# Where the rotary tables' loads stand in the preparation of a two-layer encoder trunk

## The chip, the cores and the metric

The kernel runs on one core of a Trainium2 chip. The metric is the device time of one execution in microseconds (us). Before the change it is 1481.55 us, the median of three runs (1478.82, 1481.55 and 1482.13). The engines are called as in the profile: PE is TensorE's matmul, PEld its weight load, DVE is VectorE, ACT is ScalarE, POOL is GpSimd, and SP is SyncE, which computes nothing here and issues nearly all DMAs. Each engine has a queue of its own and works it off in its written order; semaphores hold an instruction back until what it needs is there.

## The reference

The kernel computes a trunk of two encoder layers over 1024 tokens of width 1024, with a memory of 256 tokens. What matters for this change is the first layer's input side:

```python
memn = rmsnorm(mem, mem_norm_gain)
h = rmsnorm(x, norm_gain[l])
mk, mv = jnp.split(memn @ w_mem_kv[l], 2, axis=-1)
qa, ka, va, qb, kb, vb, qm, gate = split_cols(h @ w_in_even[e], SPLIT_EVEN)
qa = rope_2d(rmsnorm(qa.reshape(B, S, A_HEADS, HEAD_DIM), q_norm_a[e]), grid_row, grid_col)
ka = rope_2d(rmsnorm(ka.reshape(B, S, A_KV, HEAD_DIM), k_norm_a[e]), grid_row, grid_col)
ya = global_gqa(qa, ka, va.reshape(B, S, A_KV, HEAD_DIM))
```

`rope_2d` turns each half of a head's 64 numbers by angles that depend on the token's row and column of a 64-wide grid. The kernel doesn't compute the angles: tables of their cosines and sines (128 x 8 x 64 numbers each) are inputs, and so are the gains of the per-head norms. The rest of the layer (a global, a windowed and a memory attention, a gate, an output projection), the second layer and the final norm come after the stage that is changed.

## The kernel before

**Number format.** All products are made of 32-bit numbers split in two parts. A weight tile is loaded raw; ScalarE copies it to the high part (`wh`, L125 by way of `wparts`), VectorE or GpSimd subtracts that from the raw tile to get the low part (`wl`, L160), and TensorE makes three matmuls of each product (high by high, high by low, low by high).

**The preparation** is `project_a` (the phase named "prep"). In the order of the program it does this:

- `quarter(q, ...)` for q = 0 to 3 loads the transposed tokens a quarter at a time (`x<-xq`, L956), multiplies them by the norm's gain and splits them; `a_unit(ws, q)` multiplies a quarter by the weights of A's keys and values (L864). `quarter(4, ...)` does the same for the transposed memory (`x<-mq`). The last of these loads is kept in `self.loaded`.
- `mem_keys(w0, ...)` makes the memory's keys of layer 0: four heads of two weight units each, eight units in all, two heads to a PSUM bank (`pj`, then `tr`; matmuls at L568). `mem_values(w0, ...)` makes the values from eight more units (matmuls at L597).
- `rope_tables()` loads the factors (`so<-g_kq`, L777: four rows of 64 numbers spread over all partitions) and the two tables (`rt<-c_cos` and `rqn<-c_sin`, both L781), and GpSimd multiplies each table by the key's and by the query's factors (L784, four instructions on 128 x 512 numbers). The results, `c_cosk`, `c_cosq`, `c_sink` and `c_sinq`, are read by `rope` (L893, L895) for each quarter of keys and queries.
- `rstd(io["mt"], ...)` loads the token-major memory in four pieces (`xt<-mt`, L814; a tag of three buffers), squares and sums each on ScalarE (L815), and makes 1 / rms of the memory's tokens. `mem_keys` and `mem_values` are finished with it.
- `a_weights(1)` loads and splits the weights of A's first queries: two units into buffers of the tag `x` (L844), two into `wraw`. `stats(range(4))` does for the first four blocks of the token-major x what `rstd` does for the memory (`xt<-xt`, L814, eight pieces).
- Then follow the evictions, the rotary embedding of keys (`k_unit`) and queries (`q_unit`), the second layer's memory keys and values, and the other statistics.

**What sets the order.** The framework's planner sorts the instructions of each engine ahead of time: it runs a model of the chip, and gives each engine, whenever it is free there, the ready instruction that comes first by program order; `ahead("w")` moves a weight unit's load and split 40 places forward. A load is ready only when its buffer is free in that model. The order so found is the order in which the engine runs on the chip, where each instruction waits for its semaphores. The raw weight tiles share four buffers (`wraw`), and so do the high and the low parts (`wh`, `wl`), so a unit's load waits for the split of the unit four places before.

**`behind()`** is the only thing that was written by hand about the order of these loads: inside it, an instruction on SyncE is placed behind `self.loaded` in SyncE's queue (an order in the queue, no wait). `wload` appends each raw load to `self.raws`. The first four (`raws[0]` to `raws[3]`) are the weights of A's keys and values, and `raws[4]` to `raws[11]` are the eight units of the memory's keys. So `raws[6]` is their third and `raws[9]` their sixth. The lines around the change are in `project_a`; `rope_tables`, `rstd`, `a_weights` and `wload` all read `self.loaded` at the moment when they are traced.

Of the kernel before, what the change touches and what calls it, by code (L numbers as in the profile page):

```python
# [64 lines left out]
class Trunk:  # L65
# [881 lines left out]
    def project_a(self, qa, ks, v, qd, mem_h, kvd):  # L947


        nc, tc, io = self.nc, self.tc, self.io  # L950

        def quarter(q, parts, kps=range(4)):
            for kp in kps:
                x = self.st("x", [128, 2, 256], pool=self.xp)
                src = io["xq"][q, kp] if q < 4 else io["mq"][kp]
                loaded = nc.sync.dma_start(x, src.rearrange("p (a n) -> p a n", a=2))  # L956
                for i in range(2):
                    kt = 2 * kp + i
                    self.with_gain(x[:, i, :], kt + (0 if q < 4 else 16), *parts(kt))
            return loaded  # L960

        def tokens(q):
            return lambda kt: tuple(t[kt][:, q * 256:(q + 1) * 256] for t in self.h)
        late = []

        def after(end):

            late.append(end)
            if len(late) > 1:
                flush()  # L970

        def flush():
            with tc.issue_after(self.last.ins):
                late.pop(0)()

        warm = self.st("rp", [128, 512], F32R)
        self.st("so", [128, 512])
        self.st("rt1", [128, 512])
        nc.gpsimd.memset(warm.bitcast(F32), 0.0)
        nc.scalar.activation(self.rs_m, warm.bitcast(F32)[:, :2], AF.Sqrt)  # L980
        p = [self.ps("pj") for _ in range(2)]
        for i in range(9):
            nc.tensor.matmul(p[i % 2], warm[:, :128], warm, start=True, stop=True)
        w0, w1m = io["w_mem0"], io["w_mem1"]
        mem_l = self.st("mem", [128, KT, MEM], F32R, pool=self.xp)
        mem = [[t[:, i, :] for t in mem_h for i in range(4)], [mem_l[:, i, :] for i in range(KT)]]
        ws = self.a_weights(0, lambda kp: quarter(0, tokens(0), [kp]))
        units = []
        for q in range(4):
            units.append(self.a_unit(ws, q))  # L990
            if q < 3:
                quarter(q + 1, tokens(q + 1))
        self.loaded = quarter(4, lambda kt: (mem[0][kt], mem[1][kt]))
        for q, a in enumerate(units):
            units[q] = self.st("x", [128, 2, 256], pool=self.xp)
            self.copy(units[q], a)
        self.wsplit = ("act", "dve")
        end = [self.mem_keys(w0, mem, kvd[0], ("pj", "tr"), "so", "rt1")]
        self.wsplit = ("act", "both")
        end.append(self.mem_values(w0, mem, kvd[0], "so"))  # L1000
        self.rope_tables()
        vm = self.st("xv", [128, 2])
        self.loaded = self.raws[6]
        self.rstd(io["mt"], [0, 1], vm, self.rs_m)
        self.wsplit = ("act", "dve")
        w1 = self.a_weights(1)
        self.stats(range(4))
        self.loaded = None
        self.along_columns(self.rows_m, self.rs_m)
        for e in end:  # L1010
            e()
        for q in range(2):
            after(self.k_unit(units[q], q, ks, v))
        self.mem_keys(w1m, mem, kvd[1], ("tr", "tr"), "so", "rt1")()
        self.stats(range(4, 8))
        for q in range(2, 4):
            after(self.k_unit(units[q], q, ks, v))
        for q in range(4):
            after(self.q_unit(self.a_unit(w1, q), q, 0, qa, qd))
        w2 = self.a_weights(2)  # L1020
        self.along_columns(self.rows, self.rs)
        for q in range(4):
            after(self.q_unit(self.a_unit(w2, q), q, 2, qa, qd))
            if q == 1:
                self.mem_values(w1m, mem, kvd[1], "so")()
        while late:
            flush()
        return self.mem_q(io["w_e"], E_QM)
# [1239 lines left out]
```

## Time and profile before

| what | value |
|---|---|
| median of three runs | 1481.55 us |
| the profiled execution's own time | 1482.22 us |
| its span, from the first to the last instruction | 1480.4 us |
| TensorE busy | 1461.3 us (99%) |
| VectorE busy | 1038.8 us (70%) |
| ScalarE busy | 839.2 us (57%) |
| GpSimd busy | 647.0 us (44%) |
| moved by DMA | 271.87 MB, 184 GB/s in the mean |
| granted TensorE clock | 0.998 |

The profile is one execution of the program, taken by the hardware's profiler. Its page gives busy times for the whole span. For a single stage one asks the trace for smaller things: the busy time of each engine in chosen stretches, what an engine waited for, and the instructions of one engine in order of time. In such a row the first number is the start in us from the beginning of the span, the second how long it took (several equal instructions in a row are merged, with their count behind an x), and the brackets tell how long the engine had been idle before and which instruction or DMA ended that. For SyncE a row is the issue of a DMA, not its transfer; a view of DMA issues gives the time from the issue to the landing. A matmul's end is modelled, so that matmuls overlap in the rows; what counts is when they start.

### The profile page before, as it was taken

The numbers are of one execution on the slowest core, as the hardware profiler recorded it, in microseconds if no ns is written. First come the engines' busy times: TensorE is split into PE (matmuls) and PEld (weight loads), VectorE is DVE, ScalarE is ACT, GpSimd is POOL, SyncE is SP. The second block draws the span as 40 slices with busy tenths as digits, with TensorE's granted clock in tenths as the row PEclk, the third lists the DMA queues.
The fourth block names the chain that finished last, engine by engine and source line by source line (L and its number), as shares of the span: only waits on it lengthen the run. The fifth ranks groups of instructions, "written<-read, shape, count | busy, mean of one in ns | idle before, by whom it ended". The sixth has DMA issues, their size and how long they took to land.

```text
span 1480.4 us, 24751 instructions
## 1 busy us (share of the span) xinstructions
PE 1461.3 (99%) x8049; PEld 1254.1 (85%) x8049; DVE 1038.8 (70%) x2125; ACT 839.2 (57%) x1877; POOL 647.0 (44%) x766
## 2 busy tenths in 40 slices
PE   9999999999999999999999999999999999999997
PEld 8898888888888888888888887888888888888776
DVE  6687777777776678776687866654457787778584
ACT  7743665556655466655454544444456777776454
POOL 1223658566775656553450000002425556665355
PEclk9999999999999999999999999999999999999999
DMA  8966335334342524378553343567675568778844
GB/s 282 314 161 184 117 114 168 122 122 132 117 144 79 199 75 139 110 263 313 182 180 135 136 136 139 156 171 256 225 257 169 187 198 270 246 250 313 306 132 150
DMA packets 171809, 271.87 MB, mean 184 GB/s; under 512 B 15648, under 2 KB 92704, under 8 KB 170656
## 3 DMA queue, kind: packets, MB, share of 16 engines
q1 hardware_dynamic: 171248, 270.20, 56.6%
q8 instruction: 64, 1.05, 0.3%
q14 instruction: 65, 0.53, 0.1%
q10 hardware_dynamic: 432, 0.09, 0.0%
HBM read 174.28 MB, written 83.89 MB: 174 GB/s over the span
## 4 chain that ended last, share of the span: by engine, by line
PE 87%; DMA 4%; DVE 4%; ACT 2%; issue 1%; SPq 1%; POOL 0%; DVEq 0%; ACTq 0%; POOLq 0%
PE pj L242 16%; PE pj L62 12%; PE x L1650 7%; PE tr L133 6%; PE pv L1080 4%; PE y L1650 4%; PE pv L62 3%; PE s L62 3%; PE sa L1348 3%; PE tr L62 3%; PE pj L1348 2%; PE pv L1650 2%; PE sa L1046 2%; PE sa L1047 2%; PE s L1348 2%; PE tr L1348 2%
## 5 line engine op out<-in xcount | busy, mean ns | idle before, releaser
L549 DVE TENSOR_TENSOR pl<-tr,ph 128x512 fp32r<-128x512 f32 (+2 forms) x352 | 204.3, 594 | 45.2 <-ACT ph L125 43.3
L242 PE MATMUL pj<-H,wh 128*128 128x512 f32 x704 | 233.4, 412 | 0.4 <-DVE vt L313 0.2
L125 ACT ACTIVATE ph<-tr 128x512 fp32r<-128x512 f32 (+2 forms) x352 | 176.8, 523 | 99.6 <-PE tr L133 77.8
L158 POOL TENSOR_SCALAR wh<-wraw 128x512 fp32r<-128x512 f32 x48 | 30.4, 636 | 268.0 <-PE x L1650 233.2
L125 ACT ACTIVATE wh<-wraw 128x384 fp32r<-128x384 f32 (+1 forms) x163 | 89.2, 554 | 98.5 <-PE pj L1348 11.8
L242 PE MATMUL pj<-H,wl 128*128 128x512 f32 x352 | 139.0, 395 | 0.0
L242 PEld LDWEIGHTS pj<-H,wh 128*128 128x128 f32 x704 | 120.2, 189 | 18.2 <-issue 0.6
L62 PE MATMUL pj<-H,wh 128*128 128x512 f32 x384 | 121.0, 396 | 0.0
L1133 POOL TENSOR_SCALAR pn<-pn,st 128x384 f32<-128x384 f32 (+1 forms) x128 | 72.9, 572 | 99.3 <-DVE st L1132 57.5
L133 PE MATMUL tr<-ident,P 128*128 128x128 f32 x752 | 115.3, 273 | 0.8 <-DVE pl L549 0.5
L1295 POOL TENSOR_TENSOR wl<-wraw,wh 128x384 fp32r<-128x384 f32 x56 | 63.5, 1135 | 89.7 <-ACT wh L125 78.7
L1131 ACT ACTIVATE pn<-pn,st 128x384 f32<-128x384 f32 (+1 forms) x128 | 75.1, 587 | 40.4 <-DVE st L1128 38.9
L133 PEld LDWEIGHTS tr<-ident,P 128*128 128x128 f32 x752 | 88.8, 140 | 9.5 <-DVE pl L549 1.8
L1052 ACT ACTIVATE P<-sa,st 128x1024 f32<-128x1024 f32 x64 | 71.5, 1117 | 34.4 <-DVE st L1051 16.9
L1054 POOL TENSOR_SCALAR P<-P,st 128x1024 f32<-128x1024 f32 x64 | 73.8, 1155 | 27.5 <-DVE st L1053 27.2
L1051 DVE TENSOR_REDUCE st<-sa 128x1 f32<-128x1024 f32 x64 | 77.5, 1218 | 8.0 <-PE sa L1047 7.4
L62 PE MATMUL s<-k,q 128*128 128x384 f32 (+1 forms) x352 | 81.4, 327 | 0.7 <-DMA k<-k 0.7
L242 PEld LDWEIGHTS pj<-H,wl 128*128 128x128 f32 x352 | 66.2, 188 | 15.2
L62 PE MATMUL pj<-H,wl 128*128 128x512 f32 x192 | 75.6, 394 | 0.0
L160 POOL TENSOR_TENSOR wl<-wraw,wh 128x512 fp32r<-128x512 f32 x52 | 71.3, 1373 | 9.6 <-ACT wh L125 7.2
L62 PEld LDWEIGHTS pj<-H,wh 128*128 128x128 f32 x384 | 66.6, 188 | 5.4
L864 PE MATMUL pj<-ah,H 128*128 128x256 f32 x384 | 70.7, 282 | 0.3 <-ACT ah L125 0.2
(574 smaller groups left out, 4170.0 us busy)
## 6 DMA issues: line engine op xcount, KB each, us to landing
y<-yb SPq DMA_DIRECT2D x24, 512.0 KB, 3.9
wraw<-s SPq DMA_DIRECT2D x64, 192.0 KB, 3.8
wraw<-w_e SPq DMA_DIRECT2D x44, 256.0 KB, 3.5
k<-k SPq DMA_DIRECT2D x42, 256.0 KB, 5.5
s<-bias SPq DMA_DIRECT2D x56, 192.0 KB, 2.0
wq<-w_o SPq DMA_DIRECT2D x40, 256.0 KB, 3.3
y<-sg SPq DMA_DIRECT2D x18, 512.0 KB, 3.5
wraw<-w_o SPq DMA_DIRECT2D x36, 256.0 KB, 4.3
```

The lines of the kernel that those rows point to most:

```text
L62: return lambda *a, **k: self.tc.keep_in_program_order(getattr(self.engine, name)(*a, **k))
L125: return self.nc.scalar.activation(out, in_, AF.Copy, scale=scale)
L133: self.turned = self.fence = self.pe.transpose(o, i, self.ident)
L242: self.pe.matmul(a[:, :n], s[:, kt % UNIT, :], m, start=(kt == 0 and i == 0), stop=(kt == KT - 1 and i == 2))
L549: self.low = nc.vector.tensor_tensor(pl[:, :n], tr[:, :n], ph[:, :n], op=OP.subtract)
L1051: nc.vector.tensor_reduce(st[:, 0:1], s, axis=AX.X, op=OP.max, negate=True)
L1052: nc.scalar.activation(pt, s, AF.Exp, bias=st[:, 0:1], accum_out=st[:, 1:2])
L1054: self.normal = nc.gpsimd.tensor_scalar(pt, pt, st[:, 2:3], 0.5, op0=OP.mult, op1=OP.mult)
L1131: nc.scalar.activation(o, o, AF.Exp, bias=st[:, 0:1], scale=-1.0, accum_out=st[:, 2:3])
L1133: self.normal = normal = nc.gpsimd.tensor_scalar(o, o, st[:, 3:4], 0.5, op0=OP.mult, op1=OP.mult)
L1348: last = nc.tensor.matmul(bank, s[:, k, :], y[3 * u + k][m][:, cols], start=start and u + k + e == 0, stop=u == 1 and k + e == 4, skip_gro ...
L1650: self.last = nc.tensor.matmul(bank, ws[s][:, k, :], b[k][m], start=start and k + i == 0, stop=k == UNIT - 1 and i == 2, skip_group_check= ...
```

## The change

`rope_tables()` moves from its place ahead of the memory's statistics to a place behind them, and `self.loaded` is set to `raws[9]` just before it.

```diff
         end.append(self.mem_values(w0, mem, kvd[0], "so"))
-        self.rope_tables()
         vm = self.st("xv", [128, 2])
         self.loaded = self.raws[6]
         self.rstd(io["mt"], [0, 1], vm, self.rs_m)
+        self.loaded = self.raws[9]
+        self.rope_tables()
         self.wsplit = ("act", "dve")
         w1 = self.a_weights(1)
         self.stats(range(4))
```

Before, the three loads of `rope_tables` stood behind the last load of the transposed memory, and the loads of the memory's token-major pieces, of `a_weights(1)` and of `stats(range(4))` behind `raws[6]`. After, the memory's token-major pieces still stand behind `raws[6]`, and the loads of `rope_tables`, of `a_weights(1)` and of `stats(range(4))` stand behind `raws[9]`. In the program's order the tables now come after the memory's statistics. No instruction is added or taken away, and the sizes stay as they are. Since the planner sorts anew, the order of other instructions can change with it.

## The prediction

> **What bounds the kernel now.** I read the page's busy times first, then busy times by stretch for the preparation, then what TensorE waited for, then the order in time of the queues that feed it. The key units, the weight tiles of the first memory projection, are called K1 to K8 here (`raws[4]` to `raws[11]`), the value units behind them V1 to V8; m1 to m4 are the four loads of the token-major memory. So `raws[6]` is K3 and `raws[9]` is K6.
>
> ```profile
> span 1480.4 us, 24751 instructions
> PE 1461.3 (99%) x8049; PEld 1254.1 (85%) x8049; DVE 1038.8 (70%) x2125; ACT 839.2 (57%) x1877; POOL 647.0 (44%) x766
> ```
>
> TensorE is the bound: it is idle for 1480.4 - 1461.3 = 19.1 us in all, and a change that touches no matmul can win only some of that. The stretches (columns: length, busy time and count for each engine, granted clock, DMA share, GB/s) show where the preparation's part of it lies.
>
> ```profile
> 29.00:34.80 5.80, 5.80 (x51) 5.75 (x49) 0.69 (x1) 1.63 (x5) 4.11 (x4) 1.00 0.98 360
> 34.80:40.40 5.60, 3.44 (x23) 2.68 (x22) 2.48 (x9) 4.57 (x12) 0.92 (x1) 1.00 0.94 277
> 40.40:44.00 3.60, 3.60 (x30) 3.32 (x28) 1.75 (x3) 2.95 (x8) 1.35 (x1) 1.00 0.92 269
> 44.00:46.00 2.00, 1.74 (x9) 1.34 (x9) 0.69 (x1) 1.78 (x5) 0.84 (x1) 1.00 1.01 325
> 46.00:60.00 14.00, 14.00 (x80) 12.05 (x78) 11.34 (x38) 11.37 (x31) 4.87 (x5) 1.00 1.05 345
> 60.00:62.00 2.00, 1.64 (x12) 1.24 (x11) 1.19 (x3) 1.89 (x6) 1.17 (x2) 1.00 0.95 346
> 62.00:110.00 48.00, 48.00 (x387) 46.61 (x386) 38.82 (x100) 23.72 (x55) 10.15 (x10) 1.00 0.72 195
> ```
>
> Two things are to be seen. The hole lies at 34.8 to 40.4: 51 matmuls took 5.80 us just before it (0.114 us each), and 23 + 30 = 53 took 9.2 us from 34.8 to 44.0, where 53 x 0.114 = 6.0 would have done. So **3.2 us** is lost in the second bank of keys (K5 to K8), 2.16 of it as plain idle time. And the DMA share is 0.92 or more from 29 to 62 us: in this stage the DMA engines are full, and a load comes earlier only where another comes later. The clock is 1.00 throughout.
>
> The waits and the queue say what the hole waits for (first row TensorE; then SyncE, whose times are issues; then the subtract on VectorE that frees K1's buffer; then ScalarE; last SyncE's issue of K4 and the DMA issues of single moments, the final number from issue to landing).
>
> ```profile
> 36.66 0.39 PE L568 MATMUL tr<-q,wh 128*128 128x256 f32 x1 [1.71 <-ACT wh L125]
> 20.88 1.85 SPq L138 DMA_DIRECT2D wraw<-w_mem  x4
> 22.77 0.43 SPq L777 DMA_DIRECT2D so<-g_kq  x1
> 23.25 0.44 SPq L781 DMA_DIRECT2D rt<-c_cos  x1
> 23.74 0.65 SPq L781 DMA_DIRECT2D rqn<-c_sin  x1
> 24.43 2.69 SPq L814 DMA_DIRECT2D xt<-mt  x3
> 27.62 2.60 SPq L138 DMA_DIRECT2D wraw<-w_mem  x3
> 32.64 0.33 SPq L814 DMA_DIRECT2D xt<-mt  x1
> 33.06 0.94 SPq L138 DMA_DIRECT2D wraw<-w_mem  x1
> 34.09 1.87 SPq L814 DMA_DIRECT2D xt<-xt  x2
> 36.01 0.90 SPq L844 DMA_DIRECT2D x<-w_a  x2
> 38.30 0.33 SPq L814 DMA_DIRECT2D xt<-xt  x1
> 38.73 1.20 SPq L138 DMA_DIRECT2D wraw<-w_mem  x2
> 26.27 0.69 DVE L160 TENSOR_TENSOR wl<-wraw,wh 128x512 fp32r<-128x512 f32 x1
> 31.89 0.63 ACT L815 ACTIVATE xt<-xt 128x512 f32<-128x512 f32 x1 [2.68 <-DMA xt<-mt]
> 34.89 0.63 ACT L815 ACTIVATE xt<-xt 128x512 f32<-128x512 f32 x1 [1.58 <-DMA xt<-mt]
> 35.99 0.62 ACT L125 ACTIVATE wh<-wraw 128x512 fp32r<-128x512 f32 x1
> 22.30 0.43 SPq L138
> wraw<-w_mem SPq DMA_DIRECT2D x1, 256.0 KB, 5.9
> wraw<-w_mem SPq DMA_DIRECT2D x1, 256.0 KB, 7.9
> ```
>
> K5's matmuls wait for its copy at 35.99. That copy is written on ScalarE behind the squares of m1, m2, m3, and m3's square starts when m3 lands, 34.89. K5 itself, issued at 27.62, lands 7.9 us later, at 35.5. Both, m1 to m3 and K5, stand in the DMA queue behind the three rotary loads of 22.77 to 24.39.
>
> **The change part by part.** *The three rotary loads leave their place* ahead of m1. K4, issued at 22.30, lands 5.9 us later at 28.2; m1 lands at 31.9 (its square starts then). That is 3.7 us for four loads, 640 KB of tables and gains and m1's 256 KB. At the queue's best rate here, 360 GB/s, 256 KB take 0.7 us, which leaves **3.0 us** for the rotary loads. So m1, m2, m3 and K5, K6 can land up to 3.0 us earlier. SyncE gains 24.39 - 22.77 = 1.6 us of issue time, too. K5's issue cannot move much: it needs the buffer of K1 (four of the tag), whose subtract ended at 26.27 + 0.69 = 26.96. So m3 lands near 31.9, K5 near 32.5, its copy ends near 33.2, and TensorE, which is done with K4 at 34.8, finds it ready. The 1.71 us wait and the slow refill behind it, 36.66 - 34.80 = 1.9 us together, go: **-1.9**.
>
> *The loads come back behind K6.* They and their issues (1.6 us) now stand ahead of K7 or K8, m4, and all that follows; the planner writes which. The queue being full, K7 and K8 then land about when they do now: K7 at 36.8, K8 at 38.2.
>
> ```profile
> 29.89 0.33 SPq L138 DMA_DIRECT2D wraw<-w_mem  x1
> wraw<-w_mem SPq DMA_DIRECT2D x1, 256.0 KB, 6.9
> wraw<-w_mem SPq DMA_DIRECT2D x1, 256.0 KB, 5.1
> wraw<-w_mem SPq DMA_DIRECT2D x1, 256.0 KB, 4.9
> ```
>
> (K7 29.89 + 6.9, K8 33.06 + 5.1, V1 38.73 + 4.9 = 43.6.) With a copy and a subtract of 0.6 to 0.7 us each, K7 is ready at 38.1 and K8 at 39.5. TensorE would want them at 34.8 + 2 x 1.4 = 37.6 and near 39.3, so it waits about 0.5 us for the one, hardly for the other, and ends the bank near 41.2 instead of 44.0. Of the 3.2 us the other 1.3 us is made up of such waits, and about 0.9 of it goes: **-0.9**.
>
> *What is late next* is V1. It lands at 43.6 now and starts TensorE at 44.37. If it stays behind the same bytes, TensorE waits from 41.2 to about 43.8 and keeps only 0.6 us. But V1's buffer is that of K5, free from about 34 instead of 37.3 (35.99 + 0.62 + 0.69), and its issue at 38.73 came behind five 256 KB loads (two of `w_a`, three of `xt`) that it can now overtake at 0.7 us each, up to 3.5 us. From both sides, 0 to 2.6 us return; between ends so far apart I take the side of the saturated queue, a little over half: **+1.4**. A like bound stands at 60 to 62 us, where TensorE is idle for 0.36 us again; the same bytes are due by then, and the 1.4 that is left is about what the emptier moments of the queue (share 0.92 to 0.98) can yield.
>
> *`self.loaded` is K6 instead of K3* for the two `w_a` loads and the `xt` loads too. They are issued from 34.09 on, all behind K8 already, so the new bound costs nothing; it only keeps them from filling the place that falls free.
>
> *The four POOL multiplications* (L784) move from 30.69 to about 35.5.
>
> ```profile
> 30.69 1.29 POOL L784 TENSOR_TENSOR c_cosk<-rt,so 128x512 f32<-128x512 f32 x1 [29.43 <-DMA rt<-c_cos]
> 34.44 1.28 POOL L784 TENSOR_TENSOR c_sinq<-rqn,so 128x512 f32<-128x512 f32 x1
> 42.39 1.35 POOL L850 TENSOR_TENSOR al<-x,ah 128x512 fp32r<-128x512 f32 x1 [6.67 <-PE tr L568]
> 45.16 1.30 POOL L160 TENSOR_TENSOR wl<-wraw,wh 128x512 fp32r<-128x512 f32 x1 [1.42 <-ACT wh L125]
> 58.63 0.42 DVE L893 TENSOR_TENSOR rt<-rqn,c_cosk 128x256 f32<-128x256 f32 x1
> L796 DVE SCALAR_TENSOR_TENSOR iq_y<-iq_t,iq_y x2: 155/155/155, 57.1 to 57.2; 128x4 f32<-128x4 f32 x2
> L796 DVE SCALAR_TENSOR_TENSOR rs<-iq_t,rs x1: 1068/1068/1068, 55.2 to 55.2; 128x4 f32<-128x4 f32 x1
> ```
>
> Four of 1.29 us, 5.2 in all, would end near 40.7, still inside POOL's idle time before 42.39, and their reader at 58.63 is 18 us off. Now they run while VectorE stands idle (0.69 us busy in 29 to 34.8); then they meet its subtracts for K6 to K8. The last two rows tell what a meeting costs: the same small operation took 1.07 us instead of 0.16 at 55.2, while POOL had a subtract of its own. Between 0 and three meetings of 0.9 us each, 2.7; since TensorE has slack for some I take nothing for it in the sum and leave it to a rival.
>
> [...]
>
> **Sum**: -1.9 - 0.9 + 1.4 = -1.4 us. The profiled execution took 1482.22 us (span 1480.4 and 1.8 around it), 0.67 above the median of 1481.55; so 1480.8 in its terms and 1481.55 - 1.4 = **1480.2** against the runs. TensorE has no idle time from 62 to 110 us that could swallow the gain.
>
> **The rivals.** *The wait only moves.* V1, or the planner placing loads so that K5 and m3 keep their times: the full DMA queue speaks for it, the buffer that comes free earlier against it. Nothing changes: 1481.5. *All of it is kept.* The planner lets V1 and its followers overtake the `xt` loads: 3.2 us, with the 0.26 at 44 and the 0.36 at 60 us, 3.8 in all: 1477.7. *Slower: the tables come late on POOL.* If their loads are issued behind m4 and some `xt`, they land at 42 to 43; POOL runs in its written order, so the multiplications fill 42.5 to 47.7, and V2's subtract, now at 45.16, starts near 48.5 to 49, some 3.5 us late; TensorE is 14.00 of 14.00 busy from 46 on and has no cover. With two meetings on VectorE (1.8) less a gain of 1.9 it is +3.4: 1485.0. It decides from a landing of the tables after about 37 us (37.2 + 5.2 = 42.4). For it: the planner's order doesn't see the real queue; against: once K6 is issued, the tables rank ahead of `w_a` and `xt`.
>
> **How the numbers follow.** Chances: the forecast 0.44, the wait only moves 0.12, all is kept 0.22, slower 0.22 (with whatever a changed order does later in the program). 0.2%, which is about what a measurement of this kernel can tell from no change, is 3.0 us: faster is below 1478.6, slower above 1484.5. The forecast's own range is 1478.2 to 1481.6; 0.07 of its 0.44 count as faster. "All is kept" gives 0.21 to faster; "slower" gives 0.18 to slower and the rest to no change. So faster 0.28, same 0.54, slower 0.18. The range 1476.8 to 1485.0 leaves out about a tenth on either side.
>
> **What would show it.** Right: SyncE issues m1 to m3 directly behind K4, m1's square starts near 29, the 1.71 us wait at 36.66 is gone, and a part of it is found again at the first value matmul (L597) as a wait for `wh`. Wrong: K5 still lands after 34.8; multiplications of L784 after 42 us; subtracts of L160 well over the 0.69 us they take now; or a time that moves by more than 4 us, which no wait of this stage can pay for and which would have to come from an order changed further on.

## The result, and the profile after

The kernel after takes **1486.53 us** in the median of 18 executions (1484.2 to 1491.48), the kernel before, run beside it, 1482.46 us (18 executions, 1478.03 to 1487.56). The ratio is **1.0033, with a 95% interval of 1.0022 to 1.0044**: the change makes the kernel slower, by about 4.9 us (0.0033 x 1482.46; the two medians alone lie 4.1 apart). The forecast was 1480.2 with a range up to 1485.0.

The profiled execution of the kernel after took 1491.48 us, 4.9 us above its median, so that its numbers are somewhat larger than the typical ones; two more profiles of it stand below. The page's first lines:

```profile
span 1489.6 us, 24755 instructions
PE 1464.0 (98%) x8049; PEld 1257.6 (84%) x8049; DVE 1046.4 (70%) x2125; ACT 836.4 (56%) x1877; POOL 647.9 (43%) x766
```

TensorE's idle time is 1489.6 - 1464.0 = 25.6 us instead of 19.1. The same stretches as before (length, busy time and count of PE, PEld, DVE, ACT and POOL, granted clock, DMA share, GB/s):

```profile
34.80:40.40 5.60, 3.50 (x25) 3.09 (x26) 4.06 (x7) 4.76 (x12) 3.61 (x3) 1.00 0.85 295
40.40:44.00 3.60, 0.38 (x4) 0.17 (x2) 3.56 (x3) 2.41 (x7) 3.60 (x4) 0.85 0.23 60
44.00:46.00 2.00, 1.53 (x7) 1.53 (x8) 2.00 (x2) 0.00 (x0) 1.55 (x1) 0.50 0.18 44
46.00:60.00 14.00, 14.00 (x73) 12.42 (x73) 8.28 (x18) 9.52 (x24) 3.82 (x3) 0.87 0.97 301
```

The second row is the loss. TensorE starts 4 matmuls in 3.6 us (30 before), while VectorE is busy for 3.56 of the 3.60 us with only three instructions, and GpSimd for all of it. The DMA share falls to 0.23 and 0.18: the next loads wait for buffers, not the engines for data (from 36 to 46 us SyncE waits 6.2 us in two pieces, one of 4.9, for VectorE's subtracts). The waits of TensorE, the two rows of the timeline that make them up, and ScalarE's rows ahead of the first:

```profile
PE tr L568 <- DVE wl L160: 3.9, 2, 3.7
PE tr L568 <- ACT wh L125: 2.4, 1, 2.4
```

```profile
36.66 0.39 PE L568 MATMUL tr<-q,wh 128*128 128x256 f32 x1 [2.40 <-ACT wh L125]
44.47 0.58 PE L568 MATMUL tr<-q,wl 128*128 128x256 f32 x1 [3.69 <-DVE wl L160]
```

```profile
35.36 0.63 ACT L815 ACTIVATE xt<-xt 128x512 f32<-128x512 f32 x1 [5.15 <-DMA xt<-mt]
35.99 0.61 ACT L125 ACTIVATE wh<-wraw 128x512 fp32r<-128x512 f32 x1
```

K5's copy starts at 35.99, as before. K5 itself is there long before: SyncE issues it at 26.29, and the DMA issue of that moment lands 3.2 us later, at 29.5.

```profile
26.29 1.02 SPq L138 DMA_DIRECT2D wraw<-w_mem  x2
wraw<-w_mem SPq DMA_DIRECT2D x1, 256.0 KB, 3.2
```

But ScalarE's written order has the square of m4 ahead of K5's copy now (before, it stood behind it), and m4 lands at 35.3. The second and larger wait is for K7's low part. VectorE's rows and GpSimd's for the same time:

```profile
36.63 0.69 DVE L160 TENSOR_TENSOR wl<-wraw,wh 128x512 fp32r<-128x512 f32 x1 [0.16 <-ACT wh L125]
37.24 0.16 DVE L793 RECIPROCAL rs_m<-iq_t 128x2 f32<-128x2 f32 x1
37.32 1.71 DVE L160 TENSOR_TENSOR wl<-wraw,wh 128x512 fp32r<-128x512 f32 x1
38.95 1.24 DVE L794 TENSOR_TENSOR iq_t<-rs_m 128x2 f32<-128x2 f32 x1
40.23 1.21 DVE L795 SCALAR_TENSOR_TENSOR iq_t<-iq_t,xv 128x2 f32<-128x2 f32 x1
41.48 1.19 DVE L796 SCALAR_TENSOR_TENSOR rs_m<-iq_t,rs_m 128x2 f32<-128x2 f32 x1
42.59 1.83 DVE L160 TENSOR_TENSOR wl<-wraw,wh 128x512 fp32r<-128x512 f32 x1
44.34 1.76 DVE L850 TENSOR_TENSOR al<-x,ah 128x512 fp32r<-128x512 f32 x1
```

```profile
36.79 1.69 POOL L784 TENSOR_TENSOR c_cosk<-rt,so 128x512 f32<-128x512 f32 x1 [35.53 <-DMA xt<-xt]
38.45 1.73 POOL L784 TENSOR_TENSOR c_cosq<-rt,so 128x512 f32<-128x512 f32 x1
40.13 1.29 POOL L784 TENSOR_TENSOR c_sink<-rqn,so 128x512 f32<-128x512 f32 x1
41.37 1.28 POOL L784 TENSOR_TENSOR c_sinq<-rqn,so 128x512 f32<-128x512 f32 x1
```

The same three small operations and K7's subtract in the kernel before, when GpSimd was idle:

```profile
39.63 0.16 DVE L794 TENSOR_TENSOR iq_t<-rs_m 128x2 f32<-128x2 f32 x1
39.83 0.16 DVE L795 SCALAR_TENSOR_TENSOR iq_t<-iq_t,xv 128x2 f32<-128x2 f32 x1
40.02 0.16 DVE L796 SCALAR_TENSOR_TENSOR rs_m<-iq_t,rs_m 128x2 f32<-128x2 f32 x1
40.17 0.69 DVE L160 TENSOR_TENSOR wl<-wraw,wh 128x512 fp32r<-128x512 f32 x1
```

Now the two engines take turns. L794, on 128 x 2 numbers, ends at 38.95 + 1.24 = 40.19, when the second multiplication ends (38.45 + 1.73 = 40.18); L795 ends at 41.44 with the third (41.42), L796 at 42.67 with the fourth (42.65). Each of these three small operations lasts until a multiplication of GpSimd is done, and K7's subtract stands behind all three in VectorE's order. I call each of these a meeting. K7's own subtract (1.83) met not a multiplication but GpSimd's next instruction, a split `al` at 42.60. Not every instruction is held: the reciprocal L793 took its 0.16 us at 37.24, beside the first multiplication.

### The profile page after: what moved, and what is told of

Same layout as the page of the kernel before. It is cut to its first block, busy times and chain, and to the rows that moved or that the text cites. A ratio compares the mean times of both kernels' runs of the same rounds, so it can differ in the third digit from the quotient of the medians.

```text
span 1489.6 us, 24755 instructions
## 1 busy us (share of the span) xinstructions
PE 1464.0 (98%) x8049; PEld 1257.6 (84%) x8049; DVE 1046.4 (70%) x2125; ACT 836.4 (56%) x1877; POOL 647.9 (43%) x766
## 3 DMA queue, kind: packets, MB, share of 16 engines
q8 instruction: 64, 1.05, 0.3%
## 4 chain that ended last, share of the span: by engine, by line
PE 85%; DVE 6%; DMA 4%; ACT 2%; issue 2%; POOL 1%; SPq 0%; DVEq 0%; POOLq 0%; ACTq 0%
PE pj L242 16%; PE pj L62 11%; PE x L1651 6%; PE tr L133 6%; PE pv L1081 4%; PE y L1651 4%; PE pv L62 3%; PE s L62 3%; PE sa L1349 3%; PE tr L62 3%; PE pj L1349 2%; PE pv L1651 2%; PE s L1349 2%; PE sa L1047 2%; PE sa L1048 2%; PE tr L1349 2%
## 5 line engine op out<-in xcount | busy, mean ns | idle before, releaser
L549 DVE TENSOR_TENSOR pl<-tr,ph 128x512 fp32r<-128x512 f32 (+2 forms) x352 | 204.3, 594 | 44.7 <-ACT ph L125 42.7
L1132 ACT ACTIVATE pn<-pn,st 128x384 f32<-128x384 f32 (+1 forms) x128 | 75.1, 587 | 40.7 <-DVE st L1129 39.1
L160 POOL TENSOR_TENSOR wl<-wraw,wh 128x512 fp32r<-128x512 f32 x52 | 70.7, 1362 | 13.0 <-ACT wh L125 10.6
```

The costliest lines, as they stand in the source:

```text
L549: self.low = nc.vector.tensor_tensor(pl[:, :n], tr[:, :n], ph[:, :n], op=OP.subtract)
L1132: nc.scalar.activation(o, o, AF.Exp, bias=st[:, 0:1], scale=-1.0, accum_out=st[:, 2:3])
```

## The experiments

Two reasons were on the table. **Meetings**: the four table multiplications, which now run at 36.8 to 42.7, hold VectorE. **Order**: the planner sorted anew, and what it wrote otherwise (m4's square ahead of K5's copy, later loads) costs the time, whatever GpSimd does. (The first expectations call them the port theory and the square theory; "port" is a bare name there, and no run shows one.) Times are ratios to the kernel before, run on the same chip beside each. For the key bank itself two moments are read from each trace: the first matmul of K5 and the first of V1 (the first row of L568 into `tr` and the first of L597).

**Parts and cures of the change.** *The move alone*, with the bound left at `raws[6]`:

```diff
         self.rstd(io["mt"], [0, 1], vm, self.rs_m)
-        self.loaded = self.raws[9]
         self.rope_tables()
```

> The move without the new bound: the tables' loads stand behind the third piece of the memory, ahead of K5, and every other order is that of before. Port theory (the loss comes from the four multiplications on GpSimd meeting VectorE's work at 37 to 44 us): the tables land near 32 us, the multiplications run while VectorE is idle, as before; no subtract of L160 over 0.8 us, ratio to before 0.998 to 1.001. Square theory (the loss comes from the fourth piece's square standing ahead of K5's copy on ScalarE): the square stands behind the copy again, so also 0.998 to 1.001. If the mere later landing of the tables, or more than this stage, makes the loss: 1.002 or more.

Measured: ratio 1.0004 (0.9995 to 1.0012). The written orders are those of the kernel before but for the six loads on SyncE (m1 to m3 first, then the three tables, then K5). K5's copy isn't waited for (K6's is, 0.27 us), the multiplications run from 32.1 to 37.5, and V1 starts at 42.75 instead of 44.37. Two meetings remain, against the expectation that no subtract would take over 0.8 us: K5's subtract took 1.15 us at 34.01, and L817, on 128 x 2 numbers, 0.99 instead of 0.17 at 36.57; TensorE waited 0.79 us for K6's low part. In that execution the gain was gone at 143 us, where TensorE stood 0.1 us ahead of the kernel before: a weight unit issued earlier landed no earlier. So the bound at K6, which I costed at nothing, is what makes the change slower; the move itself costs nothing and, in time, wins nothing that shows.

*The four multiplications on VectorE*, a try to end the meetings, and the same edit on the kernel before as a control:

```diff
-                nc.gpsimd.tensor_tensor(t, raw, g[:, 2 * i + j, None, :].to_broadcast([128, 8, 64]), op=OP.mult)
+                nc.vector.tensor_tensor(t, raw, g[:, 2 * i + j, None, :].to_broadcast([128, 8, 64]), op=OP.mult)
```

> The changed kernel with the four multiplications on VectorE. Port theory: the wait of 3.7 us for K7's subtract goes, four multiplications of about 0.7 us come on VectorE, and most of the loss goes: ratio 0.999 to 1.0015. Square theory: the fourth piece's square still stands ahead of K5's copy, the wait of about 2.4 us for that copy stays and with it the loss: 1.0025 to 1.004. Both: between them, 1.001 to 1.0025.

> The kernel before, with its four table multiplications on VectorE instead of GpSimd, as a control of that edit: there VectorE is busy for only 0.69 of 5.8 us when they run, so all theories that lay the change's loss on meetings at 36 to 45 us expect no change, ratio 0.9995 to 1.0005. If moving these instructions is worth something by itself (later work on GpSimd freed, or VectorE's share made larger), it shows here as a ratio off 1 by more than 0.0007, and the run of the kernel after with this edit has to be read against it.

Measured: 1.0017 (1.0004 to 1.0030) on the kernel after, but **1.0034 (1.0022 to 1.0047)** on the kernel before, where nothing was to be cured. The edit costs time by itself: in the control TensorE waits 1.51 us at 32.24 for a low part that stands behind two multiplications on VectorE, and TensorE loses more at 98 to 156 us, where its own order and VectorE's are written otherwise. Which of the two makes up the 0.34% wasn't settled. As a test of the meetings this edit is inconclusive, here and where it was combined with others.

*The square of m4 behind K7's copy*, which takes the other suspect away (the lines that collect the copies in `self.highs` are left out here):

```diff
-                nc.scalar.activation(t, t, AF.Square, accum_out=part[:, i, j:j + 1])
+                self.squared += 1
+                with self.tc.issue_after(self.highs[6].ins) if self.squared == 4 else nullcontext():
+                    nc.scalar.activation(t, t, AF.Square, accum_out=part[:, i, j:j + 1])
```

> The changed kernel with the fourth piece's square put behind K7's copy on ScalarE. Square theory: K5's copy runs as soon as K5 lands, the wait of 2.4 us at K5 goes and the ratio falls to 0.999 to 1.002. Port theory: the multiplications still meet the subtracts of K6 to K8 and the four small steps of the memory's 1 / rms, TensorE still waits 2 to 4 us for a subtract, and the ratio stays at 1.002 to 1.004.

Measured: 1.0038 (1.0025 to 1.0051), no better than the kernel after. K5 now starts at 34.57 without a wait, 2 us earlier, and V1 still at 45.75: the chain of the memory's statistics has moved back with the square. It meets the last multiplication (which ends at 42.88) and the two splits behind it on GpSimd, as VectorE's rows show.

```profile
41.85 1.05 DVE L794 TENSOR_TENSOR iq_t<-rs_m 128x2 f32<-128x2 f32 x1
42.93 1.20 DVE L795 SCALAR_TENSOR_TENSOR iq_t<-iq_t,xv 128x2 f32<-128x2 f32 x1
44.17 1.19 DVE L796 SCALAR_TENSOR_TENSOR rs_m<-iq_t,rs_m 128x2 f32<-128x2 f32 x1
```

But V1 is only 1.8 us later there than in the mean of the kernel before (below), and the ratio stands for 5.6: most of this run's loss comes behind the key bank, where its orders are others again, and its cause wasn't followed.

*A fourth buffer for `xt`*, so that m4 lands with m1 to m3:

```diff
-... x=6, xt=3, rt1=2, ...
+... x=6, xt=4, rt1=2, ...
```

> The changed kernel with four buffers of the tag xt instead of three: the fourth piece is loaded right behind the third, its square doesn't hold K5's copy, and the memory's 1 / rms is done before the tables land. Both theories: both waits go, the bank of K5 to K8 starts at 34 us or earlier without a hole, ratio 0.996 to 1.000. If the loss is neither of the two but the order of the loads behind K6 itself: TensorE waits about as long in the same bank, 1.002 or more.

Measured: 1.0005 (0.9995 to 1.0015). The loss is gone within the interval. Here the chain runs ahead of the multiplications, and its operations are short again:

```profile
32.30 0.16 DVE L794 TENSOR_TENSOR iq_t<-rs_m 128x2 f32<-128x2 f32 x1
32.49 0.16 DVE L795 SCALAR_TENSOR_TENSOR iq_t<-iq_t,xv 128x2 f32<-128x2 f32 x1
32.69 0.16 DVE L796 SCALAR_TENSOR_TENSOR rs_m<-iq_t,rs_m 128x2 f32<-128x2 f32 x1
```

The profiled execution (1487.12 us, 4.7 above the median of that kernel) had its own trouble, K7's copy behind a split of `w_a`, 2.43 us of waiting for a low part, and V1 at 47.27; so the trace is a poor picture of the typical run, and I rest only the order and the three short rows on it.

*Both cures together*, each with the multiplications on VectorE:

> The kernel after, with both suspected causes taken away: the square of m4 stands behind K7's copy on ScalarE, and the four table multiplications run on VectorE. Theory 'order and meetings together': the square's place and the meetings of GpSimd with VectorE hide each other, so that either alone gave back half or nothing, and both together give back all: 1480 to 1482.5, ratio 0.999 to 1.001. Rival 'meetings alone': the square's place is worth nothing, as in the run with the square moved; ratio 1.0017 as with the multiplications moved alone. Rival 'the loads': the loss comes from the place of the tables' loads in the queue, which stay: ratio 1.003.

> The kernel after with four buffers of xt instead of three (m4 no longer waits for m1's square, lands early, and its square leaves K5's copy alone), and the table multiplications on VectorE. 'Order and meetings together': no hold is left, K5 to K7 come up to 2 us earlier than before, and the time is 1479.5 to 1482, ratio 0.9985 to 1.0003. 'The fourth buffer alone was enough': as without the move to VectorE, 1.0005. Rival 'VectorE has no room': the four multiplications hold its subtracts of K6 to K8 as GpSimd did, ratio 1.0015 or more.

Measured: 1.0045 (1.0030 to 1.0060) and 1.0006 (0.9996 to 1.0016). With the control above, neither tells the theories apart.

**A second profile of the kernel after.**

> The kernel after once more, for a second profile beside the same runs of the kernel before. Its first profile was 4.9 us above its median. Theory: the waits at 36 to 46 us (2.4 for K5's copy, 3.7 for a subtract held by GpSimd) and the half clock behind them stand in every execution, so this profile has them too: ratio 1.0033, half clock for 3.4 to 6.8 us from about 43. Rival: the half clock belongs to the first profile alone; then it is missing here, and the loss at 60 us is 2 us or less.

Measured: 1.0031 (1.0018 to 1.0045); the profiled execution took 1485.94 us. The meetings are there as in the first profile, and the wait behind them is 2.55 us. A second loss shows at 64 us, a meeting again: GpSimd and VectorE each have an `al` split, GpSimd's from 64.00 to 65.27, VectorE's takes 1.77 us instead of 0.68, and TensorE waits 1.5 us for it. The row of its waits, and VectorE's:

```profile
PE pj L864 <- DVE al L850: 1.5, 1, 1.5
```

```profile
64.04 1.77 DVE L850 TENSOR_TENSOR al<-wraw,ah 128x512 fp32r<-128x512 f32 x1
```

**Taking the meetings away, and putting them where they were not.** The order of work had changed in most of the runs so far. The next two edits leave it as it is on all engines; the second adds one instruction on GpSimd. *Fills*: in the kernel after, each multiplication becomes a fill of the same tile, which reads nothing; then the same on the kernel before, as a control.

```diff
-                nc.gpsimd.tensor_tensor(t, raw, g[:, 2 * i + j, None, :].to_broadcast([128, 8, 64]), op=OP.mult)
+                nc.gpsimd.memset(t, 1.0)
```

> The kernel after, with each of GpSimd's four table multiplications replaced by a fill of the same tile (all ones), which reads nothing; the products with the tables are so left out and later values are other ones. The written order of every engine stays that of the kernel after. Theory 'meetings': VectorE's three small operations of the chain L794 to L796 take 0.16 us each again instead of 1.2, K7's subtract starts near 38.5 instead of 42.3, TensorE's wait of 2.5 to 3.7 us for a low part and the half clock behind it are gone, and only the wait of 1.0 to 2.4 for K5's copy stays: ratio 0.9995 to 1.0012. Rival 'order': the loss comes from what the planner wrote otherwise (m4's square ahead of K5's copy, the later loads), which is all still there: ratio 1.0025 to 1.0035.

> Control of the edit with the fills, on the kernel before: there the four multiplications run at 30.7 to 35.7, where VectorE is nearly idle, so fills in their place should change nothing: ratio 0.9993 to 1.0007. A ratio below that would mean that the multiplications cost time in the kernel before too, and the run of the kernel after with fills has to be read against it. As there, the products with the tables are left out.

Measured: **0.9998 (0.9986 to 1.0010)** on the kernel after, 0.9997 (0.9988 to 1.0006) on the kernel before. The whole loss is gone, with every load, bound and written order of the kernel after in place. VectorE's rows of the kernel after with fills:

```profile
36.94 0.67 DVE L160 TENSOR_TENSOR wl<-wraw,wh 128x512 fp32r<-128x512 f32 x1
37.53 0.15 DVE L794 TENSOR_TENSOR iq_t<-rs_m 128x2 f32<-128x2 f32 x1
37.72 0.16 DVE L795 SCALAR_TENSOR_TENSOR iq_t<-iq_t,xv 128x2 f32<-128x2 f32 x1
37.91 0.16 DVE L796 SCALAR_TENSOR_TENSOR rs_m<-iq_t,rs_m 128x2 f32<-128x2 f32 x1
38.02 0.69 DVE L160 TENSOR_TENSOR wl<-wraw,wh 128x512 fp32r<-128x512 f32 x1
```

K7's subtract starts at 38.02 instead of 42.59, and TensorE waits 0.2 us in all for a low part in this bank. m4's square stands ahead of K5's copy as in the kernel after and is waited for (1.15 us at 36.28). So the order costs nothing against the kernel before, and what the four multiplications do at that time costs all of it. They may do it in two ways: hold VectorE, or make GpSimd late. The fills take away both, since they wait for no load and run long before:

```profile
2.58 0.53 POOL L784 MEMSET c_sinq<- 128x512 f32 x1
38.98 1.49 POOL L850 TENSOR_TENSOR al<-x,ah 128x512 fp32r<-128x512 f32 x1 [35.88 <-ACT ah L125]
```

That it is VectorE is read from the trace of the kernel after: from 30 to 50 us TensorE waited for ScalarE's copy and VectorE's subtracts (the two rows above), and for nothing of GpSimd. Whether a fill beside VectorE's work would hold it, this run doesn't show.

*The multiplications late, in the kernel before*: one added GpSimd instruction copies a column of K5's high part, and the four stand behind it.

```diff
-        self.raws = []
+        self.raws, self.lows = [], []
...
-        e.tensor_tensor(lf, raw, hf, op=OP.subtract)
+        self.lows.append(e.tensor_tensor(lf, raw, hf, op=OP.subtract))
+        if len(self.lows) == 5:
+            self.mark = nc.gpsimd.tensor_copy(self.st("mark", [128, 1]), hf.bitcast(F32)[:, :1])
...
-        self.rope_tables()
+        with self.tc.issue_after(self.mark.ins):
+            self.rope_tables()
```

> The kernel before with one added instruction: GpSimd copies one column of K5's high part, and its four table multiplications stand behind that, so that they run from about 36.7 us, as in the kernel after, instead of from 30.7. Loads and written orders stay those of the kernel before. Theory 'meetings': they hold VectorE's subtracts of K5 to K7 and the chain of the memory's statistics as in the kernel after, TensorE waits 2 to 4 us for a low part, and the ratio is 1.0015 to 1.0035 without any load having moved. Rival 'order': nothing changes but POOL's time, 0.9995 to 1.0007.

Measured: 1.0007 (0.9999 to 1.0016); between the two expectations, and not apart from no change. In the profiled execution K5 landed early (32.48), so that the multiplications began at 34.28 and not at 36.7, and the first ran beside an idle VectorE. The others held it as in the kernel after (a split `al` that met GpSimd's own came on top), and TensorE waited 4.1 us in three pieces for low parts:

```profile
PE tr L570 <- DVE wl L160: 4.1, 3, 1.7
```

```profile
35.62 1.20 DVE L819 TENSOR_SCALAR xv<-xv 128x2 f32<-128x2 f32 x1
37.53 1.06 DVE L796 TENSOR_TENSOR iq_t<-rs_m 128x2 f32<-128x2 f32 x1
38.62 1.20 DVE L797 SCALAR_TENSOR_TENSOR iq_t<-iq_t,xv 128x2 f32<-128x2 f32 x1
```

(Lines of this kernel behind L160 stand two lower.) From K5's first matmul to V1's it needs 10.56 us in this execution, where the kernel before needs 7.7 to 8.3: the held instructions make that with every load in its old place in the order. Since K5 came early there, V1 starts at 45.38, only 1.4 us later than in the mean of three executions of the kernel before (below), which is of the size of the ratio.

**The half clock.** In the kernel after the granted clock falls to 0.5 at 42.92, within the wait (0.50 at 44 to 46 us above). To see what that costs, 16 matmuls by a tile of zeros fill the wait for K7's low part (the two lines that make the tile are left out here):

```diff
+                            if banks == ("pj", "tr") and t and i and not u + k and e == 2:
+                                for _ in range(16):
+                                    nc.tensor.matmul(p[:, MEM:2 * MEM], wh[:, 0, :], self.zero, start=False, stop=False,
+                                                     skip_group_check=True)
```

> The kernel after, with 16 matmuls by a tile of zeros (added into K7's sum, so that they change nothing) just ahead of the matmul that waits 2.5 to 3.7 us for K7's low part. At 0.117 us each they fill up to 1.9 us of that wait. Theory 'the half clock follows from idle time': what is left idle there is 0.7 to 1.8 us, and the granted clock stays at 1.00 at 43 us (in the runs so far it fell after one idle stretch of 2.1 us or more, and not after one of 1.7): 15 to 30 matmuls at 0.12 instead of 0.21 us, 1.4 to 2.8 us less on TensorE at 50 us than in the kernel after. Rival 'the clock falls for another reason at that place': half clock for 3.4 us or more from about 43. The order of work behind 47 us differs a little from that of the kernel after, so that the whole time (expected 1.0020 by the theory, 1.0031 by the rival) tells less than the clock.

Measured: the clock stays at 1.00 through the preparation, as the theory expected, and the time is 1.0037 (1.0025 to 1.0049), not better at all. The time that the half clock took is now a longer wait for K8's low part, 1.68 us at 45.32 where the second profile of the kernel after had 0.44:

```profile
41.96 0.39 PE L572 MATMUL tr<-q,wl 128*128 128x256 f32 x1 [0.71 <-DVE wl L160]
45.32 0.39 PE L572 MATMUL tr<-q,wl 128*128 128x256 f32 x1 [1.68 <-DVE wl L160]
```

**More profiles of the same kernels.** The largest term of the sum rested on one execution.

> The kernel before once more, for a second profile of it. Theory 'the wait is one execution's': K5 lands between 32.4 and 36.1, the wait for its copy is anything from 0 to 2.3 us, and TensorE's first value matmul starts between 43 and 45.3. Rival 'the wait is the kernel's own': K5 lands at 35 to 36, TensorE waits 1.5 to 2 us for its copy and starts the value matmuls at 44.4 within 0.3.

> The kernel before a third time, as the run before; the two theories expect the same of it as of that run, and together they give three profiles of one kernel, in which the spread of K5's landing (3.6 us in the runs with this order so far) either shows again or doesn't.

> The kernel after a third time. Theory 'meetings': K5 lands by 31 whatever the queue does, the three small operations L794 to L796 take 1.0 to 1.25 us each, K7's subtract starts later than 41.5, and TensorE waits over 2 us for a low part and starts the value matmuls at 47 to 49.5. If the wait depended on how the queue ran, it would be missing in about one of three executions.

> The move alone a second time. If its gain in the key bank is real, TensorE's first value matmul starts at 42.5 to 43.2 again. If the gain is given back by a weight unit that lands late near 100 us in one execution only, TensorE stands 1.5 us or more ahead of the profile of before at 131 us this time; if by something that stands in the kernel, it is within 0.5 us of it there.

Measured: K5 landed at 35.20 and 34.17 in the two further profiles of the kernel before (35.51 in the first). The first rows of K5 there, in that order:

```profile
36.34 0.39 PE L568 MATMUL tr<-q,wh 128*128 128x256 f32 x1 [1.70 <-ACT wh L125]
```

```profile
34.96 0.39 PE L568 MATMUL tr<-q,wh 128*128 128x256 f32 x1 [0.56 <-ACT wh L125]
```

So the wait of 1.7 us stood in two of three executions, and the rival that it is the kernel's own is refuted by the third. The third profile of the kernel after has K5 at 31.2, the three small operations at 1.24, 1.22 and 1.19 us, and K7's subtract at 43.00; its wait for that low part is 1.53 us, less than the 2 us expected, because the clock was at half while K5 was multiplied (37.3 to 40.7) and TensorE came later. The move alone gained again, V1 at 41.68, and this time kept it: 2.2 us ahead of the kernel before at 143 us. All of these in one table (us from the start of the span; the last column is the time for which the clock was at half in the key bank):

| kernel | K5 starts | V1 starts | between | half clock |
|---|---|---|---|---|
| before | 36.66 | 44.37 | 7.71 | none |
| before, second | 36.34 | 44.35 | 8.01 | 3.4 |
| before, third | 34.96 | 43.23 | 8.27 | none |
| before, fills | 37.22 | 45.27 | 8.05 | 3.4 |
| after | 36.66 | 49.40 | 12.74 | 6.8 |
| after, second | 36.42 | 47.75 | 11.33 | 3.4 |
| after, third | 37.10 | 48.43 | 11.33 | 3.4 |
| after, zero matmuls | 35.27 | 46.60 | 11.34 | none |
| after, fills | 36.28 | 42.55 | 6.27 | none |
| before, late multiplications | 34.82 | 45.38 | 10.56 | none |
| move alone | 35.08 | 42.75 | 7.67 | none |
| move alone, second | 34.57 | 41.68 | 7.11 | none |

The three kernels after start V1 at 48.5 in the mean, the three before at 44.0: 4.5 us, of the size of the 4.9 that the ratio stands for. With fills, the way from K5 to V1 takes 6.27 us and not 11.33: the meetings are worth **5.1 us** there. The kernel before with fills, where no meeting was to be had, takes 8.05 as without them.

Single executions tell less than the ratios. The matmul that starts at 159.92 us in the first profile of the kernel before (the orders of TensorE are alike again there) starts at 158.91 and 159.89 in the two others, at 165.91, 164.38 and 166.16 in the kernel after, and at 158.40 with the fills: 5.9 us later in the mean of the kernel after, 4.5 of it from the key bank. But in the kernel before with fills it starts at 163.35, with the same orders as in the kernel before.

## Why the prediction was wrong

**K5's landing: right, and more.** Forecast 32.5, measured 29.5, 30.6 and 31.2. That the rotary loads held m1 to m3 and K5 was so.

**"Its copy ends near 33.2, TensorE finds it ready": failed.** The step took the copy to follow the landing. ScalarE runs in its written order, and there the square of m4, whose load stands behind K6 on SyncE, had come ahead of the copy. The waits for K5's copy are 2.40, 1.01 and 1.80 us in the three profiles of the kernel after and 1.71, 1.70 and 0.56 in those of the kernel before: the -1.9 was not won. It didn't cost the 4.9 either; with the fills this order is still there and the ratio is 0.9998.

**"K7 is ready at 38.1 and K8 at 39.5"; meetings on VectorE "0 to three of 0.9 us each, I take nothing": the step that failed, and by the most.** Measured in the profile of after: K6's subtract 1.71 - 0.69 = 1.02 us over, the three small operations 1.24 + 1.21 + 1.19 - 3 x 0.16 = 3.16, K7's subtract 1.83 - 0.69 = 1.14. That is 5.3 us in a row, all ahead of K7's low part, which came at 44.4 instead of 38.1, though K7 had landed at 34.6 (forecast 36.8) and its copy had ended at 37.75. In the two other profiles K7's subtract took 0.68 us, and the fifth meeting is that of the `al` split behind it (1.76 and 1.77 us), ahead of K8's low part. The multiplications themselves began at 36.79, not at 35.5. Two errors are in it. The count took the subtracts alone, three of them, though the row from which I took the price was one of a small operation (1068 ns for the same form that takes 155): each of the chain's operations L794 to L796 was one more meeting, small as they are. And the slack that was to take some of it wasn't there: the chain stands between K6's subtract and K7's in VectorE's order, and TensorE had been waiting already.

L794 to L796 each end within 0.03 us of the end of a multiplication, so that a meeting here lasted to the end of GpSimd's instruction. The reciprocal took 0.16 us beside a multiplication; L817, a `TENSOR_SCALAR`, was held in the move alone (0.99 us instead of 0.17). What decides which operation is held, no run here shows.

**V1 "+1.4" and the other 0.9**: neither was put to the test in the kernel after, where V1 had long landed when TensorE came to it. With the meetings away, V1 starts at 42.55, which is 1.4 us ahead of the 44.0 of the kernel before, the -1.4 of the sum; that the sum had the rest of the stage about right is luck, since K5's wait is still in it, and V1 starts anywhere from 43.23 to 44.37 in the three profiles of the kernel before. In the time even that doesn't show (0.9998, 0.9986 to 1.0010).

**`self.loaded` at K6 "costs nothing": failed.** The move without it is at 1.0004. The bound alone was not run; together with the move it changes the order of the loads (K5 to K8 and m4 stand ahead of the two tables), and the tables land at 36.7 and 37.3 instead of 31.9 and 32.6 with the move alone. That is what puts the multiplications where VectorE is busy.

**The rivals.** "The tables come late on POOL" had the sign (1485.0) and the landing that decides (after about 37), and it had the meetings among its terms. Its place was another: V2's subtract on GpSimd, which was to be 3.5 us late, started at 43.82 and not after 45.16. By the waits of TensorE the price lay on VectorE alone. "All is kept" and "the wait only moves" are refuted by the ratio.

**The signs to look for.** For the forecast, m1 to m3 did stand directly behind K4 (issued from 22.01) and m1's square started early (27.80), but K5's wait was not gone. Against it, L160 "well over 0.69 us" came (1.71 and 1.83), and the time moved by more than 4 us, though for the most part not through an order changed further on, as I had put it, but from this stage. After it come smaller losses of the same sort, such as the `al` split at 64 us.

**What stays open.** The move alone gains 1.2 and 2.3 us at V1, against the mean of the kernel before, and its time doesn't show it. In the first execution a late unit gave the gain back at 98 to 110 us, in the second nothing did; executions of one kernel differ by several microseconds behind the preparation, and 1.0004 (0.9995 to 1.0012) leaves room for a gain of 0.7 us. No version here is faster than the kernel before by what was measured.

## What to carry to other kernels

When work on GpSimd is moved in time, count the VectorE instructions that it will now run beside, by number and not by size, and price each at what a meeting cost: here 0.5 to 1.1 us, beside GpSimd instructions that take 1.3 us alone. A chain of operations on two columns cost more here than the large subtract behind it (3.16 us against 1.14). `TENSOR_TENSOR` and `SCALAR_TENSOR_TENSOR` on 128 x 2 numbers were held (1.05 to 1.25 us instead of 0.16), and a `TENSOR_SCALAR` of that size too (0.99 and 1.20 us instead of 0.17, in the move alone and with late multiplications); the reciprocal and a `TENSOR_REDUCE` kept their 0.16 us beside a multiplication. A load that lands earlier helps only if the instruction that reads it is next in its engine's order (here K5 landed at 29.5 instead of 35.5, and its copy started at 35.99 both times), so read that order (which a planner may write anew) ahead of costing the landing. And a control of the cure on the kernel before is worth its run: the edit that put the multiplications on VectorE cost 0.34% where there was nothing to cure.

## What the runs showed of the hardware

**The half clock cost next to nothing in this bank.** In the key bank of five of the executions in the table the granted clock fell to 0.5 for 3.4 us or twice that, each time in or behind an idle stretch of TensorE (1.70 to 3.69 us), and then a matmul starts every 0.21 us instead of 0.12, as the third profile of the kernel after has it on either side of the return at 40.7:

```profile
39.91 0.41 PE L568 MATMUL tr<-q,wl 128*128 128x256 f32 x1
40.12 0.41 PE L568 MATMUL tr<-q,wh 128*128 128x256 f32 x1
...
40.98 0.28 PE L568 MATMUL tr<-q,wl 128*128 128x256 f32 x1
41.10 0.28 PE L568 MATMUL tr<-q,wh 128*128 128x256 f32 x1
```

Yet the way from K5 to V1 took 11.33 us with 3.4 us of half clock, at 37.3 in one execution and at 43.0 in another, and 11.34 with none (the zero matmuls). The first profile, with 6.8 us of half clock, took 12.74, but there K7's subtract alone was held for 1.15 us more (1.83 instead of 0.68), so that about 0.3 us is left for the clock.

What brings a fall stays open. In the first profile of the kernel after the clock was at half from 42.92 to 49.75 and again from 111.19 to 114.61 us, for 6.83 and 3.42 us. The length of an idle stretch alone doesn't decide it: one of 1.70 us, which ended at 36.34 in the second profile of the kernel before, was followed by a fall at 38.1, while one of 1.71 us in the first profile brought none, nor did the 2.40 us that ended at 36.66 in the first profile of the kernel after, where the clock stayed at 1.00 until 42.92. So the 2.1 us in the expectation of the zero matmuls is no threshold. With those matmuls in the place of idle time the clock stayed at 1.00, in one execution; how much idle time it takes, no run here shows.

**The DMA queue isn't the same in each execution.** With one order of loads, K5 landed at 35.51, 35.20 and 34.17 in three executions of the kernel before, at 36.07 in the kernel before with fills, and at 32.48 in the kernel with late multiplications, whose loads stand in the same order. A term of 2 us that rests on a landing in one profile has that uncertainty.
